# A Trainium2 trunk kernel: rounded weight parts by transfers of their own, one decay exponential a tile, and chunk inverses made one chunk ahead

## The chip, the cores and the metric

The kernel runs on one core of a Trainium2 chip. A core has a matrix engine (PE), a vector engine (DVE), a scalar engine (ACT), a third element engine (POOL) and a sync engine (SP) that only issues transfers; POOL issues transfers as well. The metric is the device time of one execution in microseconds; lower is better.

## The reference

What is computed is a two-layer trunk on 512 tokens of width 1024. Layer 0 is a time mix with a recurrent state and a convolutional FFN, layer 1 an attention (MLA) and another such FFN, each with a norm ahead of it and behind it. The change lies in the time mix, whose reference is, cut down (`xx` is the previous token minus this one, `yn` is `y` normalised by head):

```python
def _rwkv7_step(S, inp):
    r, w, k, v, a, b = inp
    sa = jnp.einsum('bhvk,bhk->bhv', S, a)
    S = S * w[:, :, None, :] + sa[..., None] * b[:, :, None, :] + v[..., None] * k[:, :, None, :]
    y = jnp.einsum('bhvk,bhk->bhv', S, r)
    return S, y
...
    xs = x[None] + xx[None] * mu[:, None, None, :]
    rkv = jnp.einsum('nbtd,nde->nbte', xs[:3], w_rkv)
    r, k, v = rkv[0], rkv[1], rkv[2]
    xw, xa, xg = xs[3], xs[4], xs[5]
    w_log = -jax.nn.softplus(-(w0 + jnp.tanh(xw @ w1) @ w2)) - 0.5
    decay = jnp.exp(-jnp.exp(w_log.astype(f32)))
    a = jax.nn.sigmoid(a0 + (xa @ a1) @ a2)
    g = jax.nn.sigmoid(xg @ g1) @ g2
    kk = (k * k_k).reshape(B, T, H, N).astype(f32)
    kk = kk / jnp.maximum(jnp.sqrt(jnp.sum(kk * kk, axis=-1, keepdims=True)), 1e-12)
    k = k * (1.0 + (a - 1.0) * k_a)
...
    seq = tuple(jnp.moveaxis(t, 1, 0) for t in (rh, wh, kh, vh, -kk, kk * ah))
...
    _, y = lax.scan(_rwkv7_step, S0, seq)
...
    bonus = (jnp.sum(rh * kh * r_k, axis=-1, keepdims=True) * vh).reshape(B, T, D)
    out = ((yn + bonus) * g).astype(x.dtype)
    return out @ w_o
```

The recurrence is computed in 8 chunks of 64 tokens. Inside a chunk it needs, for each head, the inverse of a unit triangular 64x64 matrix.

## The kernel before

Every large matmul is made of three: the weight and the activation are each split into a rounded part (`hi`) and a remainder (`lo`), and `mm3` (L131 to L133) adds lo·hi, hi·lo and hi·hi. `weight()` makes the two parts of a weight tile (1024 x 128, kept as two halves of 128x512, 256 KB each). For each half SP loads the raw half into one of 4 `wraw` places, ACT rounds it into `whi` (L82), and an engine subtracts to get `wlo` (L125): DVE in the time mix, POOL later. Six halves (three tiles) of `whi` and `wlo` are held at once. A tile's 8 steps over k are 24 matmuls.

The time mix fills the first 396 us. Its stages are, in order:

- the norm and `group(1, 0)`: three key tiles at once, fed as each of the 8 input tiles `xh`, `xl` is made; then two key tiles alone with the fp32 matmuls of the small projections (`inner`), then `group(1, 5)` with `lora` inside it, which makes the decay exponents `cs` and the rates in `bk`;
- `group(2, 0)`, two value tiles and `group(2, 5)`. Inside them, tile by tile, run `factors` (exponentials of `cs`: `ar[...,0]` holds exp of the previous token's exponent, so its 504-column exponential is read one column earlier and POOL sets the first column to one; `ar[...,1]` holds the unshifted one; `en` is the inverse; `ka` is an affine function of the rate), `key2` (the norm of `kr`, through `ps_kn`), and `ab` (small products for the triangular matrices, sent out to `s_ab`);
- `group(0, 0)` and five receptance tiles. Beside them runs `solve`, which is 2 halves of 31 steps of two DVE operations (`tm`, `s`) that invert the 32x32 diagonal blocks, the first half for chunks 0 to 3 and the second for chunks 4 to 7. `steps(n)` advances it by n steps in the code. Behind a half, transfers on POOL's queue (`s_xd`, `s_x1`) put the result in memory, and `fetch_x` loads what one chunk needs into `TB`, `LT` and `X1`. `inv1` and `inv2` (PE, tile `ps_i`, L659 and L668) complete that chunk's inverse. `bonus` (`ps_bo`) belongs to each receptance tile;
- 8 chunks: `u_step` (needs scores `lu`), scores of the next chunk (`ps_sc`), `u2_step` (needs the inverse of this chunk), `s_step`, `tokens` (`ps_tk`), `y_state`, `y_tokens`, `yt`. `gate` (`ps_g`) fills in. From chunk 5 on the first halves of the output projection `wo` fill in;
- the second halves of `wo`, 8 tiles back to back, and the first 4 weight tiles of the FFN (`win`), L131 to L133 again.

A scheduler sets the order on each engine from the order of the code and from priorities. Each engine then runs its list strictly in order, and so does each engine's transfer queue.

Of the kernel before, what the change touches and what calls it, by code (L numbers as in the profile page):

```python
# [9 lines left out]
F32 = mybir.dt.float32  # L10
# [46 lines left out]
class Trunk:  # L57
# [53 lines left out]
    def weight(self, src, n=D, m=P, prio=None, gain=None):  # L111


        out = []
        with self.tc.high_priority(offset=WP if prio is None else prio):
            for c in range(0, n, T):
                w = min(T, n - c)
                r = self.wraw(w)
                self.nc.sync.dma_start(out=r, in_=src[:, c:c + w])
                if gain is not None:  # L120
                    v = r.rearrange("q (k c) -> q k c", c=m)
                    self.tt(v, v, bcol(gain[:, c // m:(c + w) // m], m), ALU.mult)
                h, l = self.wset()
                self.act(h[:, :w], r)
                self.wlo.tensor_tensor(out=l[:, :w], in0=r, in1=h[:, :w].bitcast(F32), op=ALU.subtract)  # L125
                out += [(h[:, i:i + m], l[:, i:i + m]) for i in range(0, w, m)]
        return out
# [26 lines left out]
    def run(self):  # L154
# [40 lines left out]
        self.wlo = nc.vector  # L195
# [105 lines left out]
    def time_mix(self, nxt, cp, gt):  # L301
# [9 lines left out]
        ar = ap.tile([P, DT, NCH, 2, C], F32, name="ar")  # L311
# [7 lines left out]
        scan = t1.tile([P, T], F32, name="scan")  # L319
        w1 = lw.tile([P, D], F32, tag="w1", name="w1")  # L320
        g1 = [lw.tile([P, n], F32, tag=f"g{i}", name="g1") for i, n in enumerate((512, 768))]
        g1k = lambda o, n: g1[0][:, o:o + n] if o < 512 else g1[1][:, o - 512:o - 512 + n]
# [37 lines left out]
        def group(i, p0, pre=None, prio=GP, mid=None):  # L360

            lag = LAG
            w = [self.weight(I["wrkv"][i, p], prio=prio) for p in range(p0, p0 + 3)]
# [72 lines left out]
        qk = group(1, 0, first, prio=G0)  # L436
        for t, n in ((w1, I["w1"]), (g1[0], I["g1"][:, :512]), (g1[1], I["g1"][:, 512:]), (self.cst, I["cst"][:, :256]), (self.ident, I["cst"][:, 256:]), (scan, I["scan"])):
            nc.sync.dma_start(out=t, in_=n)
# [63 lines left out]
        nc.gpsimd.memset(ar[:, :, :, 0, 0:1], 1.0)  # L502
        self.use_log_exp()

        def factors(p):
            cp = cs[:, p, :]
            self.act(ar[:, p, :, 0, 1:C], c3(cp)[:, :, 0:C - 1], AF.Exp, scale=-CD)
# [3 lines left out]
            self.act(c3(ka), bk[:, p, :, 0, :], AF.Identity, scale=V("ka", p), bias=om[:, 48 + p:49 + p])  # L511
# [10 lines left out]
        def key2(p, kr, sq):  # L522
# [6 lines left out]
            self.tt(ar[:, p, :, 0, :], c3(kr), ar[:, p, :, 0, :], ALU.mult)  # L529
# [145 lines left out]
        def recept(p, q):  # L675
            nc.vector.tensor_copy(out=self.pc[:, :, p], in_=ar[:, p, :, 1, C - 1])
# [17 lines left out]
        for p in range(DT):  # L694
# [3 lines left out]
            steps((0, 0, 0, 7, 7, 3, 3, 3)[p])  # L698
            rp.append(recept(p, q))
            if p in (5, 7):  # L700
                fetch_x(p // 2 - 2)
                w = inv1(p // 2 - 2, bank2)
            if p == 6:
                inv2(0, w, bank2)
# [10 lines left out]
        inv2(1, w, bank2)  # L715
# [148 lines left out]
        for ch in range(NCH):  # L864
# [4 lines left out]
            if ch == 0:  # L869
                for p in range(4):  # L870
                    gate(p, 0)
            u2_step(ch, u)
            if n + 1 < NCH:
                fetch_x(n + 1)
# [7 lines left out]
            if ch < 3:  # L882
                steps((11, 12, 1)[ch])
# [3 lines left out]
            if ch in (0, 4):  # L887
                for p in range(0 if ch else 4, DT):
                    gate(p, ch // 4)
            if n + 1 < NCH:  # L890
                fetch_v(n + 1)
                w = inv1(n + 1)
            if 5 <= ch:
                fill(2)
            if n + 1 < NCH:
                inv2(n + 1, w)
# [34 lines left out]
        self.whs.append(self.open("whl2", bufs=WB - 6))  # L931

# [385 lines left out]
```

## Time and profile before

| | us |
|---|---|
| median of 3 runs | 1366.24 (1365.59 to 1367.61) |
| the profiled execution | 1370.63 |
| its span, first to last instruction | 1368.9 |
| PE busy | 1307.6 (96%) |
| DVE busy | 815.6 (60%) |
| ACT busy | 708.8 (52%) |
| POOL busy | 291.8 (21%) |
| mean granted PE clock | 0.975 |

The profile is one execution. Each engine's busy time is a share of the span, over stages with different limits, so the table says little on any one of them: views of a stretch of time tell which engine is full there and what the others wait for. A granted clock of 1.00 is 2.4 GHz and 0.50 is 1.2 GHz.

### The profile page before, as it was taken

To read this page: it belongs to the slowest core of one execution; us is meant where nothing else is said; L and a number is where in the kernel's file an instruction comes from. 1 tells how busy PE (TensorE), PEld (TensorE's weight loads), DVE (VectorE), ACT (ScalarE), POOL (GpSimd) and SP (SyncE) were. 2 spreads that over 40 slices of the span, in tenths; PEclk is the share of its full clock that TensorE was granted. 3 is DMA by queue.
4 is the path that set the end of the run, shared out by engine and by line. 5 is a ranking of instruction groups with operands and counts; after the bars stand their busy time and mean duration, and the time that the engine had idled before them with its cause. 6 is when DMAs were issued, how large, how long until landed. Compare 5 with 4: busy or idle time off the path is not lost.

```text
span 1368.9 us, 21882 instructions
## 1 busy us (share of the span) xinstructions
PE 1307.6 (96%) x8108; PEld 1077.8 (79%) x8108; DVE 815.6 (60%) x1512; ACT 708.8 (52%) x1353; POOL 291.8 (21%) x277
## 2 busy tenths in 40 slices
PE   7989997989999999999999999999999999999995
PEld 5467775878998888888888877777898888888885
DVE  7668787677797666665233887873566555541003
ACT  6699842567676444444232566674464444433231
POOL 0001421100010000000000241222355444444443
PEclk9999998899999999999999999999999999999998
DMA  6121593345533323223333145441223222233321
GB/s 208 61 77 63 169 260 90 77 106 132 170 124 124 100 94 100 98 95 92 94 98 94 44 119 116 106 106 47 78 77 101 100 93 100 99 90 93 97 77 62
DMA packets 111211, 141.41 MB, mean 103 GB/s; under 512 B 47552, under 2 KB 54592, under 8 KB 111104
## 3 DMA queue, kind: packets, MB, share of 16 engines
q1 hardware_dynamic: 107696, 129.52, 32.2%
q0 software_dynamic: 3408, 10.49, 2.4%
q8 instruction: 64, 1.05, 0.3%
q14 instruction: 43, 0.35, 0.1%
HBM read 120.31 MB, written 12.58 MB: 97 GB/s over the span
## 4 chain that ended last, share of the span: by engine, by line
PE 75%; DVE 11%; ACT 7%; issue 3%; DMA 2%; POOL 1%; SPq 0%; POOLq 0%; ACTq 0%; DVEq 0%
PE ps_in L132 11%; PE ps_in L133 11%; PE ps_in L131 11%; PE ps_out L131 7%; PE ps_out L133 7%; PE ps_out L132 7%; PE ps_pj L132 1%; PE ps_pj L131 1%; PE ps_pj L133 1%; PE ps_o L1185 1%; DVE wlo L125 1%; DVE x L220 1%; PE ps_sc L710 1%; PE ps_t L1169 1%; ACT whi L82 1%
## 5 line engine op out<-in xcount | busy, mean ns | idle before, releaser
L82 ACT ACTIVATE whi<-wraw 128x512 fp32r<-128x512 f32 (+2 forms) x411 | 249.6, 614 | 356.9 <-PE ps_out L133 132.9
L132 PE MATMUL ps_in<-xl,whi 128*128 128x512 f32 (+1 forms) x768 | 286.9, 374 | 4.8 <-DVE xl L88 4.8
L131 PE MATMUL ps_in<-xh,wlo 128*128 128x512 f32 (+1 forms) x768 | 286.8, 374 | 0.8 <-DVE wlo L125 0.7
L125 POOL TENSOR_TENSOR wlo<-wraw,whi 128x512 fp32r<-128x512 f32 (+2 forms) x176 | 221.8, 1266 | 304.4 <-ACT whi L82 299.0
L133 PE MATMUL ps_in<-xh,whi 128*128 128x512 f32 (+1 forms) x768 | 285.7, 373 | 0.0
L125 DVE TENSOR_TENSOR wlo<-wraw,whi 128x512 fp32r<-128x512 f32 x229 | 154.0, 679 | 92.7 <-ACT whi L82 90.8
L132 PEld LDWEIGHTS ps_in<-xl,whi 128*128 128x128 f32 x768 | 145.5, 190 | 31.3 <-DVE xl L88 6.3
L131 PEld LDWEIGHTS ps_in<-xh,wlo 128*128 128x128 f32 x768 | 145.3, 190 | 26.7 <-DVE wlo L125 0.9
L133 PEld LDWEIGHTS ps_in<-xh,whi 128*128 128x128 f32 x768 | 145.6, 190 | 24.8
L131 PE MATMUL ps_out<-hh,wlo 128*128 128x512 f32 (+1 forms) x396 | 146.6, 370 | 1.3 <-ACT mg L82 1.3
L133 PE MATMUL ps_out<-hh,whi 128*128 128x512 f32 (+1 forms) x396 | 145.3, 367 | 0.0
L132 PE MATMUL ps_out<-hl,whi 128*128 128x512 f32 (+1 forms) x396 | 144.1, 364 | 0.0
L85 DVE TENSOR_TENSOR macc<-macc,msq 128x512 f32<-128x512 f32 (+1 forms) x25 | 15.5, 619 | 136.1 <-ACT msq L82 136.1
L237 POOL TENSOR_TENSOR row<-row,msq 128x256 f32<-128x256 f32 x14 | 14.1, 1010 | 379.8 <-ACT msq L82 379.3
L131 PE MATMUL ps_pj<-xh,wlo 128*128 128x512 f32 x192 | 79.0, 430 | 8.6 <-ACT xh L82 6.7
L88 DVE SCALAR_TENSOR_TENSOR c<-gp,vec,c 128x512 f32<-128x512 f32 x88 | 72.6, 827 | 24.1 <-ACT c L82 22.7
L131 PEld LDWEIGHTS ps_out<-hh,wlo 128*128 128x128 f32 x396 | 74.4, 188 | 13.5 <-ACT mg L82 1.9
L133 PEld LDWEIGHTS ps_out<-hh,whi 128*128 128x128 f32 x396 | 74.3, 188 | 13.5
L132 PEld LDWEIGHTS ps_out<-hl,whi 128*128 128x128 f32 x396 | 74.3, 188 | 13.1
L132 PE MATMUL ps_pj<-xl,whi 128*128 128x512 f32 x192 | 77.2, 404 | 0.3 <-DVE xl L85 0.2
L133 PE MATMUL ps_pj<-xh,whi 128*128 128x512 f32 x192 | 76.5, 400 | 0.0
L85 DVE TENSOR_TENSOR u<-ps_in,row 128x512 f32<-128x512 f32 x44 | 30.3, 689 | 63.0 <-PE ps_in L133 63.0
(289 smaller groups left out, 2385.2 us busy)
## 6 DMA issues: line engine op xcount, KB each, us to landing
wraw<-in_win SPq DMA_DIRECT2D x176, 256.0 KB, 2.7
wraw<-in_wout SPq DMA_DIRECT2D x80, 256.0 KB, 2.6
wraw<-in_wrkv SPq DMA_DIRECT2D x48, 256.0 KB, 3.2
wraw<-in_wo SPq DMA_DIRECT2D x32, 256.0 KB, 2.9
x<-in_xT SPq DMA_DIRECT2D x16, 256.0 KB, 4.7
wraw<-in_ow SPq DMA_DIRECT2D x16, 256.0 KB, 3.1
s_ab<-ab POOLq DMA_DIRECT2D x16, 128.0 KB, 2.8
s_vt<-vT POOLq DMA_DIRECT2D x8, 256.0 KB, 2.8
```

Source lines behind the costliest of these rows:

```text
L82: self.nc.scalar.activation(out=out, in_=in_, func=func, **kw)
L85: self.nc.vector.tensor_tensor(out=out, in0=a, in1=b, op=op)
L88: self.nc.vector.scalar_tensor_tensor(out=out, in0=a, scalar=s, in1=b, op0=op0, op1=op1)
L125: self.wlo.tensor_tensor(out=l[:, :w], in0=r, in1=h[:, :w].bitcast(F32), op=ALU.subtract)
L131: mm(ps, lhsT=wl, rhs=xh, start=start, stop=False)
L132: mm(ps, lhsT=wh, rhs=xl, start=False, stop=False)
L133: mm(ps, lhsT=wh, rhs=xh, start=False, stop=stop)
L220: eng.tensor_tensor(out=xk, in0=xk, in1=mg, op=ALU.add)
L237: (self.nc.gpsimd if (h, k) in ACCP else self.nc.vector).tensor_tensor(out=self.acc2[:, c], in0=self.acc2[:, c], in1=sq, op=ALU.add)
L710: mm(qs[hd][:, p], lhsT=b, rhs=a, start=True, stop=True)
L1169: nc.tensor.transpose(out=q[:, o:o + P], in_=pr[i][:, j * P:(j + 1) * P], identity=t.ident)
L1185: nc.tensor.matmul(q[HALF[i], j * P:], lhsT=VT[pr // 4][j][:, c:c + 64], rhs=w, start=j == 0, stop=j == QB - 1)
```

## The change

1. `weight()`: while `self.cast` is set, `whi` is no longer rounded by ACT from the raw half. A transfer on POOL's queue reads the same half of the weight once more and rounds it on its way into `whi`. SP still loads the raw half, since `wlo` is made from it. This holds for the time mix's projections, the gates' weights, `wo` and the first four FFN tiles, 82 halves in all. The first group's six halves are loaded to places in the tile `art`, which is not yet used for anything else, and ACT rounds them as before. `w1`, `g1` and `scan` are put in `art` too.
2. `factors` makes one exponential of the decay, and the shifted one is gone. `before(p)` reads the unshifted one, one column earlier, after DVE has written ones into the first columns (128x8).
3. `ka` goes from ACT to DVE (`tensor_scalar`), the small copy `pc` from DVE to ACT.
4. `steps` before the chunks: 14 where there were 23, so the first half of `solve` ends there and one step of the second is done; the rest runs in chunks 0 to 2.
5. No inverse is made before the chunks. Chunk 0's is made inside chunk 0, after `u_step` and the next chunk's first scores, with the gates around it; each later chunk's at the end of the chunk before. Its `fetch_x` stands one chunk earlier than that. The second set of gates stands in chunk 4.

```diff
 
-    def weight(self, src, n=D, m=P, prio=None, gain=None):
+    def weight(self, src, n=D, m=P, prio=None, gain=None, raw=None):
 
...
         out = []
+        raw = raw or self.wraw
         with self.tc.high_priority(offset=WP if prio is None else prio):
...
                 w = min(T, n - c)
-                r = self.wraw(w)
+                r = raw(w)
                 self.nc.sync.dma_start(out=r, in_=src[:, c:c + w])
...
                 h, l = self.wset()
-                self.act(h[:, :w], r)
+                if self.cast and raw == self.wraw:
+
+                    self.nc.gpsimd.dma_start(out=h[:, :w], in_=src[:, c:c + w])
+                else:
+                    self.act(h[:, :w], r)
                 self.wlo.tensor_tensor(out=l[:, :w], in0=r, in1=h[:, :w].bitcast(F32), op=ALU.subtract)
...
             nc.vector.tensor_scalar(out=self.om[:, a:a + n], in0=self.vec[:, _VEC[nm]:_VEC[nm] + n], scalar1=-1.0, scalar2=1.0, op0=ALU.mult, op1=ALU.add)
-        self.wlo = nc.vector
+        self.wlo, self.cast = nc.vector, True
         f0, m1, f1 = FFN(self, 0), MLA(self), FFN(self, 1)
...
         ap = self.open("apool")
-        ar = ap.tile([P, DT, NCH, 2, C], F32, name="ar")
+        art = ap.tile([P, DT * NCH * 2 * C + P], F32, name="ar")
+        ar = art[:, :DT * NCH * 2 * C].rearrange("q (p c s t) -> q p c s t", p=DT, c=NCH, s=2)
         bk = ap.tile([P, DT, NCH, 2, C], F32, name="bk")
...
         lw = self.open("lw", side="right")
-        scan = t1.tile([P, T], F32, name="scan")
-        w1 = lw.tile([P, D], F32, tag="w1", name="w1")
-        g1 = [lw.tile([P, n], F32, tag=f"g{i}", name="g1") for i, n in enumerate((512, 768))]
-        g1k = lambda o, n: g1[0][:, o:o + n] if o < 512 else g1[1][:, o - 512:o - 512 + n]
+        scan = art[:, 7 * D:7 * D + T]
+        w1, g1 = art[:, 3 * D:4 * D], art[:, 4 * D:4 * D + 1280]
+        g1k = lambda o, n: g1[:, o:o + n]
         x = self.x
...
 
-        def group(i, p0, pre=None, prio=GP, mid=None):
+        def group(i, p0, pre=None, prio=GP, mid=None, raw=None):
 
             lag = LAG
-            w = [self.weight(I["wrkv"][i, p], prio=prio) for p in range(p0, p0 + 3)]
+            w = [self.weight(I["wrkv"][i, p], prio=prio, raw=raw) for p in range(p0, p0 + 3)]
             q = [self.bank("ps_pj") for _ in range(3)]
...
 
-        qk = group(1, 0, first, prio=G0)
-        for t, n in ((w1, I["w1"]), (g1[0], I["g1"][:, :512]), (g1[1], I["g1"][:, 512:]), (self.cst, I["cst"][:, :256]), (self.ident, I["cst"][:, 256:]), (scan, I["scan"])):
+        places = iter(range(2 * DT))
+
+        def staged(n):
+
+            o = next(places) * T
+            return art[:, o:o + n]
+        qk = group(1, 0, first, prio=G0, raw=staged)
+        for t, n in ((w1, I["w1"]), (g1, I["g1"]), (self.cst, I["cst"][:, :256]), (self.ident, I["cst"][:, 256:]), (scan, I["scan"])):
             nc.sync.dma_start(out=t, in_=n)
...
             kept(p, qk[p - 5])
-        nc.gpsimd.memset(ar[:, :, :, 0, 0:1], 1.0)
         self.use_log_exp()
 
+        def before(p):
+
+            nc.vector.memset(ar[:, p, :, 0, C - 1:C], 1.0)
+            o = p * NCH * 2 * C + C - 1
+            return art[:, o:o + NCH * 2 * C].rearrange("q (c s t) -> q c s t", s=2, t=C)[:, :, 0, :]
+
         def factors(p):
             cp = cs[:, p, :]
-            self.act(ar[:, p, :, 0, 1:C], c3(cp)[:, :, 0:C - 1], AF.Exp, scale=-CD)
             en = t1.tile([P, T], F32, tag="en", name="en")
...
             ka = t1.tile([P, T], F32, tag="ka", name="ka")
-            self.act(c3(ka), bk[:, p, :, 0, :], AF.Identity, scale=V("ka", p), bias=om[:, 48 + p:49 + p])
+            nc.vector.tensor_scalar(out=c3(ka), in0=bk[:, p, :, 0, :], scalar1=V("ka", p), scalar2=om[:, 48 + p:49 + p], op0=ALU.mult, op1=ALU.add)
             self.act(ar[:, p, :, 1, :], c3(cp), AF.Exp, scale=-CD)
...
             self.stt(kr, rv, 1e12, kr, ALU.min, ALU.mult)
-            self.tt(ar[:, p, :, 0, :], c3(kr), ar[:, p, :, 0, :], ALU.mult)
+            self.tt(ar[:, p, :, 0, :], c3(kr), before(p), ALU.mult)
             self.tt(bk[:, p, :, 0, :], c3(kr), bk[:, p, :, 0, :], ALU.mult)
...
         def recept(p, q):
-            nc.vector.tensor_copy(out=self.pc[:, :, p], in_=ar[:, p, :, 1, C - 1])
+            self.act(self.pc[:, :, p], ar[:, p, :, 1, C - 1])
             self.tt(ar[:, p, :, 1, :], c3(q), ar[:, p, :, 1, :], ALU.mult)
...
                 bonus(*rp.pop(0))
-            steps((0, 0, 0, 7, 7, 3, 3, 3)[p])
+            steps((0, 0, 0, 5, 5, 4, 0, 0)[p])
             rp.append(recept(p, q))
-            if p in (5, 7):
-                fetch_x(p // 2 - 2)
-                w = inv1(p // 2 - 2, bank2)
-            if p == 6:
-                inv2(0, w, bank2)
+        fetch_x(0)
+
         def score_mm(ch, g):
...
             bonus(*rp.pop(0))
-        inv2(1, w, bank2)
         gate_weights()
...
             if ch == 0:
+                w = inv1(0)
                 for p in range(4):
                     gate(p, 0)
+                inv2(0, w)
+                for p in range(4, DT):
+                    gate(p, 0)
+                fetch_x(1)
             u2_step(ch, u)
-            if n + 1 < NCH:
-                fetch_x(n + 1)
             if n < NCH:
...
             if ch < 3:
-                steps((11, 12, 1)[ch])
+                steps((11, 11, 40)[ch])
             y_tokens(ch, q)
...
                 yt(ch - 1)
-            if ch in (0, 4):
-                for p in range(0 if ch else 4, DT):
-                    gate(p, ch // 4)
+            if ch == 4:
+                for p in range(DT):
+                    gate(p, 1)
+            if n < NCH:
+                w = inv1(n)
             if n + 1 < NCH:
                 fetch_v(n + 1)
-                w = inv1(n + 1)
             if 5 <= ch:
                 fill(2)
+            if n < NCH:
+                inv2(n, w)
             if n + 1 < NCH:
-                inv2(n + 1, w)
+                fetch_x(n + 1)
             if ch == 6:
...
         self.whs.append(self.open("whl2", bufs=WB - 6))
+        self.cast = False
```

What this makes of the order is shown at three places. The first is PE at the end of the last receptance tile, where the chunks begin (`ps_i` the inverse, `ps_sc` scores, `ps_bo` the bonus, `ps_tk` tokens, `ps_u` the chunk's first product, `ps_g` gates). Before:

```order
L133 MATMUL ps_pj<-xh,whi 128x512
L710 MATMUL ps_sc<-ar,bk 128x128 x8
L659 MATMUL ps_i_2021<-s_1562 64x64 x8
L686 MATMUL ps_bo<-rkk,cst 128x512
L668 MATMUL ps_i_2087<-wi,s_1562 64x64 x8
L686 MATMUL ps_bo<-rkk,cst 128x512
L659 MATMUL ps_i_2166<-T_1793,s_1562 64x64 x8
```

After, from the same place, and then where the first inverse stands now:

```order
L701 MATMUL ps_bo<-rkk,cst 128x512
L722 MATMUL ps_sc<-ar,bk 128x128 x8
L701 MATMUL ps_bo<-rkk,cst 128x512 x2
L722 MATMUL ps_sc<-ar,bk 128x128 x8
L781 MATMUL ps_tk<-ident,bk 128x64 x16
L789 MATMUL ps_u<-v,lu_2166 64x64
```

```order
L722 MATMUL ps_sc<-ar,bk 128x128 x5
L674 MATMUL ps_i_2257<-s_1550 64x64 x8
L136 MATMUL ps_g<-gt,wlo 128x256
L137 MATMUL ps_g<-gxl,whi 128x256
L138 MATMUL ps_g<-gt,whi 128x256
L569 MATMUL ps_g<-gt,whi 128x256
```

Sixteen scores, two bonuses, the 16 token transposes and all of `ps_u` stand ahead of the first `ps_i` now, where 8 scores stood; the gates stand right behind it.

The second place is ACT inside `group(2, 0)`, around the factors of one tile (`krv` the key norm, `hm` and `xh` the group's own inputs). Before:

```order
L82 ACTIVATE ar<-cs 128x8x63
L82 ACTIVATE xh<-xs 128x512
L82 ACTIVATE hm<-h,om 128x512
L82 ACTIVATE en<-cs 128x512
L82 ACTIVATE ka<-bk,om,vec 128x512
L82 ACTIVATE xh<-xs 128x512
L82 ACTIVATE ar<-cs 128x8x64
L82 ACTIVATE kr<-bk,vec 128x512
L82 ACTIVATE ksq<-bk,vec 128x512
L82 ACTIVATE krv<-ps_kn,tiny 128x512
L82 ACTIVATE hm<-h,om 128x512
L82 ACTIVATE krv<-krv 128x512
```

After:

```order
L82 ACTIVATE en<-cs 128x512
L82 ACTIVATE ar<-cs 128x8x64
L82 ACTIVATE xh<-xs 128x512
L82 ACTIVATE hm<-h,om 128x512
L82 ACTIVATE ksq<-bk,vec 128x512
L82 ACTIVATE krv<-ps_kn,tiny 128x512
L82 ACTIVATE xh<-xs 128x512
L82 ACTIVATE krv<-krv 128x512
```

The 504-column exponential (128x8x63) and `ka` are gone from the list, and no cast of weights stands among the rest any more. Earlier on ACT, in `group(1, 5)`, one `en` stands ahead of rates that are still to come, and with it two table loads that were not there:

```order
L82 ACT_TABLE_LOAD
L82 ACTIVATE en<-cs 128x512
L82 ACT_TABLE_LOAD
L82 ACTIVATE sg<-ps_lo,vec 128x512
L82 ACTIVATE bk<-ps_lo,vec 128x8x64
```

Before, one table load stood between the last of the rates (`sg`, `bk`) and the first `en`; now an `en` is drawn in among them, and there are three.

The third place is POOL's queue, from its first transfers on. Before:

```order
L541 DMA s_ab<-ab 128x4x64 x2
L417 DMA s_vt<-vT 128x512 x2
L541 DMA s_ab<-ab 128x4x64 x2
L417 DMA s_vt<-vT 128x512 x2
L541 DMA s_ab<-ab 128x4x64 x2
```

After:

```order
L127 DMA whi<-in_wrkv 128x512 x19
L556 DMA s_ab<-ab 128x4x64 x2
L127 DMA whi<-in_wrkv 128x512 x2
L422 DMA s_vt<-vT 128x512
L127 DMA whi<-in_wrkv 128x512
L422 DMA s_vt<-vT 128x512
L127 DMA whi<-in_wrkv 128x512
```

The weights' transfers stand among those that send results of ACT out, in one queue; a transfer there waits behind the ones ahead of it.

## Rows read from the trace of the kernel before

**Rows 1.** Windows of the time mix; columns in its first row
```profile
core 0: us, PE busy (x) PEld busy (x) DVE busy (x) ACT busy (x) POOL busy (x), PEclk, DMA share, GB/s
0.00:72.00 72.00, 63.71 (x226) 36.72 (x227) 48.27 (x74) 48.77 (x77) 1.65 (x11) 0.95 0.38 128
72.00:152.00 80.00, 71.82 (x414) 53.13 (x414) 58.61 (x92) 77.02 (x133) 11.62 (x16) 0.96 0.27 88
152.00:168.00 16.00, 16.00 (x168) 12.35 (x163) 13.87 (x22) 13.23 (x25) 6.33 (x9) 1.00 0.62 188
168.00:200.00 32.00, 31.06 (x152) 25.67 (x151) 27.49 (x58) 16.82 (x30) 7.83 (x13) 1.00 0.92 253
200.00:224.00 24.00, 24.00 (x102) 18.82 (x101) 21.98 (x52) 7.42 (x11) 3.81 (x8) 1.00 0.45 130
224.00:264.00 40.00, 30.90 (x306) 23.83 (x306) 22.39 (x57) 14.47 (x29) 6.80 (x12) 0.70 0.35 80
264.00:296.00 32.00, 27.65 (x592) 24.46 (x588) 27.63 (x66) 22.46 (x50) 1.10 (x2) 1.00 0.37 87
296.00:360.00 64.00, 61.21 (x1155) 56.49 (x1154) 45.90 (x84) 45.97 (x103) 0.00 (x0) 1.00 0.56 153
360.00:396.00 36.00, 36.00 (x319) 35.88 (x316) 30.61 (x63) 27.31 (x63) 0.00 (x0) 1.00 0.50 155
```

**Rows 2.** Groups of ACT, 72 to 152 us: busy, mean ns, idle before
```profile
L82 ACT ACTIVATE whi<-wraw 128x512 fp32r<-128x512 f32 x19 | 11.6, 627 | 0.0
...
L82 ACT ACTIVATE ka<-bk,om,vec 128x512 f32<-128x512 f32 x7 | 5.6, 806 | 0.0
...
L82 ACT ACTIVATE ar<-cs 128x504 f32<-128x504 f32 x8 | 5.0, 619 | 0.0
...
L82 ACT ACT_TABLE_LOAD x2 | 2.6, 1283 | 0.0
```

**Rows 3.** What PE waited for, 72 to 152 us (us, times, longest)
```profile
PE ps_kn L524 <- ACT ksq L82: 3.6, 1, 3.6
PE ps_kn L524 <- ACT krv L82: 2.2, 1, 2.2
PE ps_pj L131 <- DVE wlo L125: 1.9, 3, 1.0
```

**Rows 4.** What PE waited for, 224 to 300 us
```profile
PE ps_i L659 <- DMA s<-s_x: 8.3, 1, 8.3
PE ps_i L659 <- issue: 1.5, 1, 1.5
```

**Rows 5.** Chain of waits, 222 to 240 us: start us, us, what
```profile
223.18 2.10 ACT s L82
...
232.43 1.69 DMA s<-s_x
```

**Rows 6.** What PE waited for, 0 to 30 us
```profile
PE ps_pj L131 <- ACT xh L82: 6.3, 1, 6.3
```

**Rows 7.** Groups of DVE, 72 to 152 us
```profile
L125 DVE TENSOR_TENSOR wlo<-wraw,whi 128x512 fp32r<-128x512 f32 x18 | 11.9, 682 | 3.6 <-ACT whi L82 3.5
...
L676 DVE COPY pc<-ar 128x8 f32<-128x8 f32 x8 | 2.4, 295 | 1.4 <-ACT ar L82 1.4
```

**Rows 8.** Issues of `s_vt` on POOL: ns min/median/max
```profile
L417 POOL DMA_DIRECT2D s_vt<-vT x8: 552/552/555, 130.7 to 177.8; - x8
```

**Rows 9.** Transfers, 72 to 152 us: KB each, median us to landing
```profile
s_vt<-vT POOLq DMA_DIRECT2D x4, 256.0 KB, 2.3
```

**Rows 10.** Projections alone, 200 to 224 us: PE, PEld, DVE, ACT
```profile
200.00:224.00 24.00, 23.11 (x96) 17.73 (x95) 2.73 (x4) 0.00 (x0) 1.00 0.45 130
```

**Rows 11.** Transfers, 160 to 224 us
```profile
wraw<-in_wrkv SPq DMA_DIRECT2D x11, 256.0 KB, 4.3
```

**Rows 12.** Output projection matmuls alone, 360 to 396 us: PE, PEld, ACT
```profile
360.00:396.00 36.00, 35.01 (x285) 34.43 (x285) 8.32 (x22) 1.00 0.50 155
```

**Rows 13.** Transfers of those 36 us: packets, MB, share of 16 engines
```profile
q1 hardware_dynamic: 3017, 5.50, 49.4%
```

## The prediction

> **What bounds the kernel now.** I read the windows table first [rows 1], to see in which stretch of the time mix PE is not full, or full at a low granted clock. PE is nearly full in most; what is lost lies in three. From 72 to 152 us it is busy 71.8 of 80 at a clock of 0.96: 8.2 us idle, and about 0.04 x 71.8 = 2.9 of slow work, 11.1 in all. From 224 to 264 it is busy 30.9 of 40 at 0.70: 9.1 idle and 0.30 x 30.9 = 9.3 slow. From 264 to 296 it is idle 4.4. Behind 296 there is little to gain: 2.8 us of 64, and nothing in the last 36.
>
> Next, who is late there. In the first stretch ACT is busy 77.0 of 80 [rows 1], and its list [rows 2] shows no idle time ahead of any group: ACT is the bound, and PE's waits are for what ACT makes [rows 3], 3.6 us for `ksq`, 2.2 for `krv`, and 1.9 for `wlo`, which waits for ACT's cast in its turn. In the second stretch PE waits 8.3 us for one transfer, the inverse's data, and 1.5 behind it [rows 4]. The chain [rows 5] tells the story: `solve`'s first half ends, ACT copies (2.10 us at 223.18), and only at 232.43 does the last load begin, since the result goes out to memory and back. The first `ps_i` stands behind 8 scores only, so PE has nothing else; after the wait the clock is low. DVE works beside it, 22.4 + 27.6 = 50.0 us of the 72 from 224 to 296 [rows 1].
>
> **The change part by part.**
>
> *Start.* The first projection waits 6.3 us for ACT's first `xh` [rows 6]. In the order of the changed kernel all six casts of the first group stand ahead of `xh`, as six did before, but five now stand behind the norm. One more operation on that path is 0.68 us on DVE (`wlo`) [rows 7]; I take +0.6, with ends -1 and +1.5.
>
> *72 to 152 us.* ACT loses 17 of the 19 casts (two belong to the small weights, which keep theirs): 17 x 0.627 = 10.7; eight exponentials, 5.0; seven `ka`, 5.6 [rows 2]. It gains two table loads, 2 x 1.283 = 2.6, and eight `pc`, no row of ACT; as on DVE 0.295 each [rows 7], 2.4. Net 16.3, so ACT falls to 60.7 of the present 80. DVE has 58.6 now [rows 1] and gets seven `ka`, between 0.295 and 0.69 by the other DVE rows, at most 4.8, loses 2.4 of `pc` and gets small memsets of less: about 61. So neither is the bound any more and PE is, with its 11.1 us of loss as the most that can be had. The three waits of [rows 3] make 7.7; the clock, with no idle stretch of 3.6 us left, may give back 2.9: 10.6 together.
>
> Against that stands a longer way to a weight. Now `whi` needs no place until the raw half is there, and a cast (0.63) and `wlo` (0.68) follow. After the change the transfer itself must wait until PE releases the place, then takes 0.55 to issue [rows 8] and 2.3 to land [rows 9], and `wlo` 0.68: 3.5 us against 1.3. A half lasts PE 12 matmuls of 23.11/96 = 0.24, 2.9 us [rows 10]. In the single tiles six halves are in hand, 17 us, and nothing shows. At the end of a group all three tiles end together, and the order has 12 matmuls between the last release and the first need: 3.5 - 2.9 = 0.6 a half at best, and if transfers queue behind one another 1.5 or so. Two group ends lie in this stretch; I take 2.5 off. **Forecast -8**, with ends -11 and 0 (all of it eaten).
>
> *152 to 224 us.* PE is full, so only loss is possible. Eleven raw halves are loaded from 160 to 224 [rows 11]; each is now read twice. One costs all sixteen transfer engines about 0.494 x 36 / 21 = 0.85 us, by the 5.50 MB (21 halves of 0.262) in the last stretch [rows 12, 13]. That is 9.4 us more in a stretch where their share is 0.92 for 32 us and 0.45 for 24 (free: 2.6 + 13.2) [rows 1]. It fits, late. Two more group ends are here. **+2**, ends 0 and +9.
>
> *224 to 296 us.* The inverse of chunk 0 now stands behind sixteen scores, two bonuses, the token transposes and `ps_u`, work that PE does today after the wait. So the 8.3 and the 1.5 are covered; where that cover is gone, they are back. With no long idle stretch the clock should not fall, 9.3 us. But then DVE is what is late next: its 50.0 us here include solve's second half, which must end before chunk 4, and none of it goes away. 72 - 50 = 22 is all that DVE leaves, and PE's own loss, 9.1 + 9.3 + 4.4 = 22.8, says the same. A serial chunk does not run DVE full: I take the waits (9.8) and somewhat under half of the clock (4.2). **-14**, ends -22 and -5.
>
> *The rest of the chunks.* Nothing before 360 changes but places; 0. Solve's last steps stand in chunk 2, and chunk 4's inverse at the end of chunk 3; the way out and back (11 us in [rows 5], from 223.2 to 234.1) has about a chunk to hide in.
>
> *The last 36 us.* `wo` matmuls take 35.01/285 = 0.123 [rows 12], so a half lasts 1.47 us, and needs 2 x 0.85 = 1.7 us of the transfer engines. 21 halves fall short by 0.23 each, 4.8; six stand ready. **+1.5**, ends 0 and +8 (the issues on POOL too, 0.55 each [rows 8], hide).
>
> A page of the Trainium skill speaks against sending weights this way: SBUF - State Buffer (the box on the "DVE blocks DMA" trap) says that a DMA from POOL's queue cannot get its descriptors while DVE runs a 2-port operation, as an fp32 copy from SBUF to SBUF is, and gives 3.1 us where 0.62 was needed. The moved `ka` would be such an operation. The trace does not show it: the eight `s_vt` issues took 552, 552 and 555 ns (least, median, most) [rows 8] while DVE was busy 73% of the stretch, though with few copies in it. By the page's figures eight such delays would cost at most 8 x 2.5 = 20 us of waiting in transfers, an estimate, most of it hidden.
>
> **Sum.** 0.6 - 8 + 2 - 14 + 1.5 = -17.9. The profiled execution took 1370.6, so it would take 1352.7; it is 4.4 above the median of 1366.2, and I set the same difference on the median: **1348.3 us**.
>
> **Rivals.**
> 1. *The transfers are late and eat the first stretch* (8 becomes 0). For it: the longer way to a weight, and one queue for weights and for ACT's results, where a weight waits behind an `s_ab` that waits for ACT. Against it: a landing of 2.3 us. 0.6 + 0 + 2 - 14 + 1.5 = -9.9: 1356.
> 2. *The inverse's wait returns inside chunk 0* (or DVE is the bound sooner): 14 becomes 5, the clock stays low. For it: DVE must end solve's first half with everything else it has there. 0.6 - 8 + 2 - 5 + 1.5 = -8.9: 1357.
> 3. *Both*: -0.9: 1365, no change that shows.
> 4. *All goes well*: -11 - 22 + 0.6 = -32: 1334.
> 5. *A DVE lock on POOL's descriptors*, priced by rows: each of eight `ka` holds a weight back by its own length, 0.69 at most, 5.5 us of the 8: 1354.
> 6. *Slower: POOL's queue carries one weight at a time in the output projection.* Then a half costs its landing, 2.3 us, or 4.3 where traffic is dense [rows 11], against 1.47. 24 halves (8 tiles of `wo` and 4 of the FFN) at 4.3 - 1.47 = 2.8 are +68, at 2.3 +20; without the 1.5 the sum is -19.4, so it decides from (19.4/24 + 1.47) = 2.3 us a half. At 3 us: 24 x 1.53 = 37 - 19 = +17: 1384. Against it: 21 hardware transfers passed in 36 us, and a landing time is not a spacing.
> That the change does not do what it says, the order excludes.
>
> **How the numbers follow.** Chances: forecast 0.46 (its own range 1340 to 1354), rival 1 0.17, rival 2 0.12, both 0.05, all well 0.07, lock 0.04, slower 0.09. Faster by more than 0.2% (2.7 us, what a measurement of this kernel can tell from no change): 0.46 + 0.17 + 0.12 + 0.07 + 0.04 = 0.86; within 0.05; slower 0.09. The range leaves out the slower case, "both", and about half of "all well", 0.18 in all: 1335 to 1364.
>
> **What would show each step.** ACT under 65 of 80 us between 72 and 152, with no wait of PE for `ksq` or `krv`: the first term. PE's waits for `wlo` there, over 4 us: rival 1. PE at a clock near 1.00 from 224 on with no wait over 2 us for `s_x`, chunk 3 some 14 us sooner against the end of the last projection: the fourth term; a wait of `ps_i` in chunk 0 is rival 2. A `ps_wo` waiting for `wlo` is rival 6. The forecast is wrong if the transfers land in more than about 5 us where a group ends, or if DVE fills the chunks.

## The result: slower

The changed kernel took 1381.6 us (median of 4, 1378.9 to 1387.8) where the kernel before took 1366.9: a ratio of 1.011, 95% interval 1.007 to 1.015. The forecast was 1348. The profiled execution of the change took 1387.8 us, 17.1 more than that of before, where the medians differ by 14.7.

I laid the two traces side by side by events of PE: the end of a projection tile, of a chunk, of a weight tile. How far the change is behind (+) or ahead (-) at each, in us, gives the terms of the sum as they came out:

| up to | before | after | behind | term | forecast |
|---|---|---|---|---|---|
| end of the first group | 38.7 | 40.0 | +1.3 | +1.3 | +0.6 |
| end of the second value tile alone | 143.8 | 149.6 | +5.8 | +4.5 | -8 |
| end of the last receptance tile | 224.8 | 237.9 | +13.2 | +7.4 | +2 |
| end of the last chunk | 366.8 | 372.8 | +6.0 | -7.2 | -14 |
| first 4 FFN weight tiles, about | 423.1 | 437.6 | +14.5 | +8.5 | +1.5 |
| last instruction | 1368.9 | 1386.0 | +17.1 | +2.6 | 0 |

The last 2.6 lie behind the code that is changed. A position comes from one profiled execution each: `e6` below, whose code is the change's up to the chunks, is +10.4 at the last receptance tile, so a difference of 3 us between two kernels' positions says little by itself. The windows of the change, which answer to [rows 1] (PE, PEld, DVE, ACT, POOL busy, granted clock, transfers' share, GB/s):

```profile
72.00:152.00 80.00, 71.99 (x414) 51.23 (x414) 61.60 (x94) 65.05 (x112) 19.72 (x33) 0.98 0.51 151
...
168.00:200.00 32.00, 29.21 (x171) 24.42 (x170) 19.37 (x41) 10.49 (x18) 13.28 (x22) 1.00 1.02 262
200.00:224.00 24.00, 20.35 (x73) 15.25 (x74) 17.43 (x37) 1.45 (x2) 4.39 (x8) 0.86 0.80 234
224.00:264.00 40.00, 35.19 (x258) 27.73 (x258) 30.98 (x81) 15.44 (x29) 11.50 (x20) 0.83 0.52 136
264.00:296.00 32.00, 28.27 (x630) 24.94 (x628) 29.15 (x72) 20.38 (x44) 0.00 (x0) 1.00 0.35 77
...
360.00:396.00 36.00, 33.76 (x371) 32.12 (x370) 21.86 (x41) 13.67 (x36) 9.52 (x18) 1.00 0.95 284
```

ACT did fall, from 77.0 to 65.1 of the 80 us from 72 to 152, and PE gained nothing by it. From 168 to 224 us, where PE had been full, it is idle 6.4 us: the transfer engines are full for the first 32 of them (1.02) and at 0.80 after that. In the last row their share is 0.95, where it was 0.50, and PE idles 2.2.

What PE waits for from 72 to 152 us, against [rows 3]:

```profile
PE ps_pj L136 <- DVE wlo L130: 4.0, 5, 2.2
PE ps_vt L428 <- ACT krv L82: 2.0, 1, 2.0
```

The waits for `ksq` are gone, and those for `wlo` have grown from 1.9 to 4.0 us. The weights' transfers there, and from 160 to 224 us (KB each, median us to landing; [rows 9, 11] before):

```profile
whi<-in_wrkv POOLq DMA_DIRECT2D x20, 256.0 KB, 3.8
wraw<-in_wrkv SPq DMA_DIRECT2D x18, 256.0 KB, 3.1
```

```profile
whi<-in_wrkv POOLq DMA_DIRECT2D x16, 256.0 KB, 4.9
wraw<-in_wrkv SPq DMA_DIRECT2D x12, 256.0 KB, 5.5
...
s<-s_ab SPq DMA_DIRECT2D x4, 256.0 KB, 7.1
```

3.8 us and then 4.9, where I had put 2.3 by `s_vt`; and the loads for the triangular matrices, `s<-s_ab`, take 7.1. One chain shows what that does. It runs from 188 to 204 us (start, length, what):

```profile
187.99 7.45 DMA whi<-in_wrkv
...
195.86 0.69 DVE wlo L130
...
199.71 0.41 DVE s L85
...
200.91 0.69 DVE wlo L130
...
202.77 0.75 DVE rkk L88
...
203.65 2.04 PE ps_bo L701 x2
```

A rounding transfer takes 7.45 us. DVE's `wlo` waits for it at 195.86. DVE runs its list in order, so `solve`'s steps and `rkk`, the bonus's input, come behind it, and `rkk` ends at 203.5. PE, whose list has the bonus in the middle of a projection, stands still.

That transfer is not the whole delay, and not the larger part. DVE's list a little earlier (start, length; in brackets how long DVE stood and for what), in the change and then, one line, in `e1`, which is the change without the rounding transfers:

```profile
188.76 0.19 DVE L85 TENSOR_TENSOR tm<-s 128x31 f32<-128x31 f32 x1 [3.76 <-DMA s<-s_ab]
...
194.50 0.69 DVE L130 TENSOR_TENSOR wlo<-wraw,whi 128x512 fp32r<-128x512 f32 x1 [2.26 <-PE ps_pj L136]
```

```profile
178.49 0.18 DVE L85 TENSOR_TENSOR tm<-s 128x31 f32<-128x31 f32 x1
```

These `tm` are `solve`'s first step. DVE stands 3.8 us ahead of it for a load of `s_ab`, then 2.3 for a place that PE holds, and 0.4 for the transfer of 7.45. The first step is 10.3 us later than in `e1`, and the first `rkk` 10.1 (202.8 for 192.6): against `e1` the delay is there when `solve` starts.

What PE waits for from 196 to 290 us, and the clock in some windows of that stretch (PE busy, clock, share, GB/s):

```profile
PE ps_bo L701 <- DVE rkk L88: 7.6, 2, 6.4
PE ps_tk L781 <- DVE sign L750: 3.6, 1, 3.6
```

```profile
200.00:204.00 4.00, 0.35 (x1) 0.79 1.10 362
204.00:208.00 4.00, 4.00 (x8) 0.50 0.98 264
...
244.00:248.00 4.00, 0.84 (x16) 0.83 0.75 169
248.00:252.00 4.00, 3.53 (x31) 0.50 0.92 235
252.00:256.00 4.00, 4.00 (x42) 0.50 0.78 178
256.00:260.00 4.00, 4.00 (x24) 0.50 0.15 27
```

The 6.4 us are most of the loss of the third term, with half clock behind them. The second stop comes at the start of the chunks. DVE there:

```profile
241.27 0.74 DVE L88 SCALAR_TENSOR_TENSOR rkk<-ar,vec,bk 128x512 f32<-128x512 f32 x1
245.72 0.09 DVE L627 MEMSET s<- 128x32 f32 x1 [3.71 <-POOL s L626]
246.93 0.19 DVE L85 TENSOR_TENSOR tm<-s 128x31 f32<-128x31 f32 x1 [1.12 <-ACT s L82]
247.03 0.68 DVE L85 TENSOR_TENSOR vTr<-ps_bo,vTr 128x512 f32<-128x512 f32 x1
...
248.33 0.14 DVE L750 COPY sign<-cst 128x1 f32<-128x1 f32 x1
```

DVE stands 3.7 us before it writes the ones for `solve`'s second half, for POOL's clearing, and 1.1 more for ACT's copy. The last bonuses (`vTr`) and the `sign` that PE's token transposes wait for are behind that in its list; PE's clock is at 0.50 from 248 to 260. The output projection shows the last loss, transfers from 360 to 410 us against [rows 13]:

```profile
q1 hardware_dynamic: 4533, 8.26, 51.5%
q0 software_dynamic: 3740, 6.81, 47.2%
...
whi<-in_wo POOLq DMA_DIRECT2D x19, 256.0 KB, 5.3
wraw<-in_wo SPq DMA_DIRECT2D x18, 256.0 KB, 5.4
```

Both queues together hold 99% of sixteen engines, and a half lands after 5.3 us.

### The profile page after: what moved, and what is told of

Same layout as the page of the kernel before. It is cut to its first block, busy times and chain, and to the rows that moved or that the text cites. A ratio compares the mean times of both kernels' runs of the same rounds, so it can differ in the third digit from the quotient of the medians.

```text
span 1386.0 us, 21956 instructions
## 1 busy us (share of the span) xinstructions
PE 1312.0 (95%) x8108; PEld 1078.1 (78%) x8108; DVE 816.5 (59%) x1520; ACT 659.7 (48%) x1263; POOL 337.2 (24%) x360
## 4 chain that ended last, share of the span: by engine, by line
PE 67%; issue 12%; DVE 9%; DMA 6%; ACT 3%; POOL 2%; POOLq 0%; SPq 0%; DVEq 0%; ACTq 0%
PE ps_in L137 11%; PE ps_in L138 11%; PE ps_in L136 11%; PE ps_out L136 7%; PE ps_out L138 7%; PE ps_out L137 7%; DMA whi<-in_wrkv 3%; PE ps_o L1203 1%; DVE x L225 1%; PE ps_t L1187 1%; DVE wlo L130 1%; PE ps_pj L137 1%; PE ps_pj L136 1%; PE ps_pj L138 1%; POOL whi L127 1%
## 5 line engine op out<-in xcount | busy, mean ns | idle before, releaser
L82 ACT ACTIVATE whi<-wraw 128x512 fp32r<-128x512 f32 (+2 forms) x321 | 194.6, 610 | 329.5 <-PE ps_out L138 132.6
L136 PE MATMUL ps_pj<-xh,wlo 128*128 128x512 f32 x192 | 78.4, 426 | 11.8 <-ACT xh L82 7.2
```

Source lines behind the costliest of these rows:

```text
L82: self.nc.scalar.activation(out=out, in_=in_, func=func, **kw)
L136: mm(ps, lhsT=wl, rhs=xh, start=start, stop=False)
```

## The experiments

Each run is given with its ratio to the kernel before on the same chip and the 95% interval; positions are those of the table above. The kernel before took 1369.5 to 1371.6 us beside these runs and 1366.9 beside the change, so kernels are compared by their ratios.

**The parts apart.** `e1` is the change with one word of it undone:

```diff
-        self.wlo, self.cast = nc.vector, True
+        self.wlo, self.cast = nc.vector, False
```

> The changed kernel with no rounding transfers: ACT casts every weight half again, each weight is read once; the single exponential, the moved ka and pc, the staged first group and the new order of solve and inverses stay. Theory T (reading each weight twice fills the transfer engines, once from 168 to 200 us and once in the output projection, and a late hi part holds up DVE, which runs in order, and PE behind it): both losses vanish, the chunks keep their 7 us of gain, so 1358 us (1352 to 1364), under the kernel before. Rival R (solve's first half, now ended later in the code, is what makes PE wait for DVE; the transfers don't matter): it stays at 1375 or more.

Measured 1355.1 us, ratio 0.988 (0.984 to 0.992): R falls. It is level with the kernel before at the last receptance tile (-0.0), 15.3 ahead at the last chunk, and stays there. So the rounding transfers alone make the difference between -15.4 and +17.1 us at the last instruction: -0.3, 5.2, 8.3, 8.1, 8.5 and 2.7 by the terms of the table. Its windows:

```profile
168.00:200.00 32.00, 31.54 (x153) 25.82 (x151) 28.36 (x62) 15.13 (x27) 7.17 (x11) 1.00 0.94 253
200.00:224.00 24.00, 24.00 (x101) 18.70 (x100) 20.66 (x49) 8.73 (x13) 6.16 (x11) 1.00 0.54 156
224.00:264.00 40.00, 37.08 (x643) 31.14 (x643) 35.05 (x86) 24.72 (x56) 4.10 (x8) 1.00 0.42 91
```

`e2` puts the transfers alone into the kernel before:

```diff
-                self.act(h[:, :w], r)
+                if self.cast and not own:
+                    self.nc.gpsimd.dma_start(out=h[:, :w], in_=src[:, c:c + w])
+                else:
+                    self.act(h[:, :w], r)
```

> The kernel before with only the rounding transfers (the first group is cast by ACT, as in the change). T: it loses the 7 to 9 us between 168 and 215 us and some 9 in the last 40 us of the time mix, without the chunks' gain: 1385 us (1378 to 1392). R: 1370 or less, or a gain.

Measured 1392.9, ratio 1.016 (1.012 to 1.020), 0.9 past the end of T's range: +11.2 at the last receptance tile, +24.7 at the FFN's first tiles. `e3` has solve's steps and the inverses moved alone:

```diff
-            steps((0, 0, 0, 7, 7, 3, 3, 3)[p])
+            steps((0, 0, 0, 5, 5, 4, 0, 0)[p])
...
-                steps((11, 12, 1)[ch])
+                steps((11, 11, 40)[ch])
```

> The kernel before with only solve's steps and the inverses moved, as in the change. T: 1360 us (1355 to 1364), 7 us off between the last projection and the last chunk, and no wait of PE for the bonus's input in the receptance tiles. R: that wait is there, and the time is 1372 or more.

Measured 1358.5, ratio 0.991 (0.988 to 0.994): T. `e4` has the single exponential, `ka` and `pc` alone:

```diff
-            self.act(ar[:, p, :, 0, 1:C], c3(cp)[:, :, 0:C - 1], AF.Exp, scale=-CD)
...
-            self.tt(ar[:, p, :, 0, :], c3(kr), ar[:, p, :, 0, :], ALU.mult)
+            self.tt(ar[:, p, :, 0, :], c3(kr), before(p), ALU.mult)
```

> The kernel before with only the single decay exponential, ka on DVE and pc on ACT (and the small table scan kept in the tile ar, for room). T: ACT, full from 72 to 152 us, loses some 9 us of work there; PE's waits for the key norms shrink: 1363 us (1359 to 1367). Rival: DVE, which gets ka and the ones, or the added table loads take it back: 1367 and no difference.

Measured 1363.9 with a spread of 1356.4 to 1369.1, ratio 0.995 (0.992 to 0.997). A gain, but of 1.6 us only at the last receptance tile; the rest comes in chunk 0, where the inverse's data are waited for 4.7 us, not 8.3, since `solve`'s first step comes at 178.5, 5.6 us earlier. Of PE's waits (60 to 224 us) `ksq` shrinks from 3.6 and `krv` stays:

```profile
PE ps_kn L529 <- ACT ksq L82: 2.4, 1, 2.4
PE ps_ab L542 <- ACT krv L82: 2.3, 1, 2.3
```

**Where the transfers cost.** `e5` ends them before `group(2, 5)`, `e6` before the output projection, `e12` leaves them out between `group(0, 0)` and the chunks. Each sets `self.cast` at that place:

```diff
+        self.cast = False
         qv = group(2, 5, mid=lambda k: keyed(9 + k // 2) if k in (0, 2) else None)
```

> The changed kernel with the rounding transfers kept only up to the second value tile alone (until about 150 us); from group(2, 5) on ACT casts. T (double reads fill the transfer engines from 168 us on and in the output projection): both losses vanish, 1364 us (1358 to 1369). Rival L (the transfers' late start behind PE's release and POOL's queue costs wherever they are used): about half of the 15 us of loss stays, 1372.

Measured 1357.3, ratio 0.990 (0.988 to 0.993), better than T asked and equal to `e1` within their intervals: the first 20 transfers, the last of them issued at 126.9 us, neither gain nor lose anything that shows.

> The changed kernel with ACT's casts again for the output projection and the FFN's first tiles, transfers elsewhere in the time mix. T: the 9 us between the last chunk and the first FFN tiles go, the loss from 168 to 215 stays: 1373 us (1369 to 1377). Rival: the last stage is late for what the chunks leave behind, not for the transfers: 1380.

Measured 1374.9, ratio 1.004 (1.002 to 1.006): the last stage's 8.5 go (+2.6 at the last chunk and at the FFN's first tiles), the rest stays, as T says.

> The changed kernel with ACT's casts for the receptance tiles and the gates' weights alone (about 180 to 230 us), transfers before and behind. T (the transfer engines were full there already): the 8 us from 197 to 213 us and the low clock in chunk 0 go, the output projection's 9 stay: 1368 us (1364 to 1372). Rival (the backlog comes from the value tiles before it): 1378.

Measured 1370.6, ratio 1.001 (0.9995 to 1.003): T. Over the receptance tiles it loses 1.2 us (from +2.3 to +3.5) where the change loses 9.0 (from +4.2 to +13.2), and it is -9.1 at the last chunk; then the output projection takes 9 back. PE's waits there:

```profile
PE ps_bo L702 <- DVE rkk L88: 1.3, 1, 1.3
...
PE ps_tk L782 <- DVE sign L751: 0.2, 1, 0.2
```

**Traffic or late start.** `e8` keeps the rounding transfer and drops the raw load:

```diff
-                self.nc.sync.dma_start(out=r, in_=src[:, c:c + w])
+                if not one:
+                    self.nc.sync.dma_start(out=r, in_=src[:, c:c + w])
```

> The changed kernel in which a weight that is rounded by a transfer is not read a second time: the raw half isn't loaded, and wlo is hi minus hi, so zero (the remainders of these weights are left out). The late start of a transfer stays, the doubled traffic goes. T: the losses from 168 to 215 us and in the output projection go with the traffic: 1365 us (1358 to 1369). L (late start): 1376 or more.

Measured 1367.2, spread 1361.4 to 1370.4, ratio 0.998 (0.996 to 0.999): in T's range, and still 1% above `e1`. From the last chunk to the FFN's tiles it loses 3.8 where the change loses 8.5; over the receptance tiles 4.9 (from -0.4 to +4.5), where the change loses 9.0. So the doubled traffic is about half of each loss. The other half is a `hi` part that is still late: DVE stands up to 2.3 us for one in the receptance tiles, and PE 1.9 for a `wlo` in the FFN's tiles. Whether it is late because the transfer can start only when PE releases the place, or because it lands slowly, isn't shown; from 168 to 200 us the transfer engines are as full here as in the change. Its share at both places, and the landing in the output projection:

```profile
168.00:200.00 32.00, 28.68 (x134) 23.34 (x133) 24.69 (x54) 7.50 (x13) 10.93 (x18) 0.95 1.03 249
...
360.00:396.00 36.00, 33.78 (x264) 33.17 (x263) 29.80 (x65) 14.94 (x39) 10.61 (x20) 0.95 0.58 156
```

```profile
whi<-in_wo POOLq DMA_DIRECT2D x14, 256.0 KB, 3.1
```

**The port lock.** `e7` puts `ka` back on ACT.

```diff
-            nc.vector.tensor_scalar(out=c3(ka), in0=bk[:, p, :, 0, :], scalar1=V("ka", p), scalar2=om[:, 48 + p:49 + p], op0=ALU.mult, op1=ALU.add)
+            self.act(c3(ka), bk[:, p, :, 0, :], AF.Identity, scale=V("ka", p), bias=om[:, 48 + p:49 + p])
```

> The changed kernel with ka on ACT again. Rival K (DVE's one-operand operation on fp32 data in SBUF locks POOL out of writing descriptors, so that weights land late): the hi parts land in 2.3 us from 72 to 152 where 3.8 is seen, and the time falls by 5, to 1377. T: they land as before, and the time is the same within 3 us, 1382.

Measured 1385.0, ratio 1.010 (1.008 to 1.012), as the change. The hi parts land there in 3.4 us, where the change has 3.8 and K asked for 2.3:

```profile
whi<-in_wrkv POOLq DMA_DIRECT2D x20, 256.0 KB, 3.4
```

So K falls: the time does not drop, and the change's 3.8 us are not `ka`'s doing but for 0.4 at most (in `e8`, with `ka` on DVE and less traffic, they land in 3.4 too). The Trainium skill's page SBUF - State Buffer (box on the "DVE blocks DMA" trap) has such an operation lock POOL out of writing descriptors while it runs. A hold of `ka`'s own length, 0.55 us, can't be told from none here.

**The chunks' missing half.** `e11` let `solve` pause behind its first half, to take its second half out of DVE's list ahead of the last bonuses.

```diff
                 nc.gpsimd.dma_start(out=self.s_x1[g], in_=sA[:64].rearrange("q a b -> q (a b)"))
+                yield
...
-                nc.vector.memset(sX.rearrange("q a b -> q (a b)")[:, ::33], 1.0)
+                (nc.gpsimd if g else nc.vector).memset(sX.rearrange("q a b -> q (a b)")[:, ::33], 1.0)
```

> The changed kernel, transfers and all, with solve paused in the same way. Theory H (with the transfers late, DVE stands still for solve's second half, with the last bonuses and the scores' masks behind it; PE then waits 3.6 us and its clock is at 0.50 for about 12 us): that wait and the low clock go, 5 to 8 us off the 1382, 1375 us (1372 to 1378). Rival: PE then waits for another late thing at the same place (the last bonus's input), 1381.

Measured 1399.9, ratio 1.021 (1.018 to 1.024). The pause also moved ACT's copy of the second half's input behind `fetch_x(0)`, which writes over it; the second half is computed from other data, and PE waits 13.9 us for the result ahead of chunk 4. It answers nothing. `e13` mends that: the copy and the clearing stay ahead of the pause.

```diff
                 if g == 1:
-                    self.act(sA, lX)
-                    nc.gpsimd.memset(s4[:, 1], 0.0)
+                    yield
...
+                if g == 0:
+                    self.act(sA, lX)
+                    nc.gpsimd.memset(s4[:, 1], 0.0)
```

> The changed kernel, transfers and all, with solve paused behind its first half: the copy and the clearing that the second half needs stay where they are, its ones are written by POOL and its first step stands in chunk 0, so none of it is ahead of the last bonuses on DVE. (The run e11 meant this, but put the copy behind the first fetch too, which overwrites what it reads, and so lengthened chunk 2; it answers nothing.) Theory H: the 3.6 us wait of PE behind DVE and the 12 us at half clock go, 5 to 8 us off, 1375 us (1372 to 1378). Rival: another late thing takes its place, 1381.

Measured 1382.7, ratio 1.009 (1.006 to 1.012): the rival. The wait for `sign` is gone, and 4.8 us for the inverse's data stand in its place:

```profile
PE ps_bo L703 <- DVE rkk L88: 8.2, 3, 6.2
PE ps_i L676 <- DMA T<-s_xd: 4.8, 1, 4.8
```

So DVE's standstill was one face of it. What lies ahead of both is that `solve`'s first half ends late. ACT's copy behind it starts in the change, and in `e1`, at (start, length):

```profile
240.26 1.99 ACT L82 ACTIVATE s<-s 64x1024 f32<-64x1024 f32 x1 [0.44 <-DVE s L85]
```

```profile
218.56 2.09 ACT L82 ACTIVATE s<-s 64x1024 f32<-64x1024 f32 x1 [2.20 <-DVE s L85]
```

The change's last projection ends at 237.9 and that of `e1` at 224.7: the copy starts 2.4 us behind it in the one and 6.1 ahead of it in the other. Over the kernels with the new order, and the kernel before: the end of chunk 0 (its `s_step`), counted from the last projection's end, and the gain on the kernel before from there to the last chunk:

| kernel | half ends, against last projection | chunk 0 ends behind it | chunks' gain |
|---|---|---|---|
| before | -1.6 | 37.7 | |
| e9 | -6.2 | 18.4 | 17.0 |
| e14 (below) | -6.2 | 18.4 | 11.2 |
| e1 | -6.1 | 18.4 | 15.3 |
| e5 | -4.1 | 19.3 | 15.8 |
| e8 | -3.1 | 26.7 | 11.9 |
| e12 | -2.2 | 22.4 | 12.6 |
| e3 | -1.4 | 23.7 | 10.7 |
| change | +2.4 | 28.4 | 7.2 |
| e7 | +2.9 | 26.8 | 11.8 |
| e6 | +3.1 | 29.0 | 7.8 |
| e13 | +3.3 | 28.8 | 8.2 |

The end of chunk 0 goes with that margin, but for `e8`, where PE waits 2.9 us for the last bonuses' input. The gain up to the last chunk follows less well, since later chunks have stops of their own: `e14` waits 6.0 us for the second half's data, and in the change PE's clock is at 0.79 from 296 to 312 us; `e7`, with the half as late, gains 11.8. No run moves the half's end by itself, so that it is the cause is argued from this table and not shown.

**A faster version.** `e9` is `e1` with the first group loaded through the usual four places:

```diff
-        qk = group(1, 0, first, prio=G0, raw=staged)
+        qk = group(1, 0, first, prio=G0)
```

> The changed kernel with no rounding transfers, and the first group's raw halves loaded through the four usual places, not through the tile ar. Theory S: the staged loads put five casts between the norm and the first input and cost 1.5 us at the first group's end (40.3 us against 38.7); without them that end is at 38 to 39, and the time 1.5 under the run e1, 1353.5 us. Rival: the loss is made up later anyway, 1355.

Measured 1351.4 (1350.4 to 1352.3), ratio 0.986 (0.984 to 0.987): the lowest of all, in an interval that overlaps that of `e1`; the first group ends at 37.9 where `e1` has 40.3. `e10` and `e14` are `e9` with the pauses of `e11` and `e13`.

> As e9, and solve pauses once its first half is sent out, so that none of the second half (its first step, and the ones that DVE writes, which POOL writes here) stands ahead of the last bonuses on DVE. Without the transfers DVE is in time there (no wait of PE for it in e1), so the same as e9 within 2 us: 1353 us.

> The run e9 (no rounding transfers, first group unstaged) with solve paused in the same way. There PE did not wait at that place, so the same as e9 within 2 us: 1351 us.

`e10` took 1367.1, ratio 0.997 (0.995 to 0.999), with the overwritten input of `e11`. `e14` took 1354.0, ratio 0.989 (0.986 to 0.992), 3 us above `e9` where no more than 2 were expected: the pause gains nothing, and its own wait, 6.0 us for the second half's data, comes in its place.

## Why the prediction was wrong, step by step

- **Start.** Sign and cause right, size 1.3 for 0.6; with the staging undone (`e9`) the first group ends 0.8 earlier than before, as it does in `e4`.
- **72 to 152 us** is the step that failed most: -8 was forecast, +4.5 came, outside its ends of -11 and 0. That ACT is full there was read rightly, and its relief came out at 12.0 us where I had 16.3. The error was to credit PE with its waits as soon as ACT has room. From the first group's end to the second value tile PE gained 0.7 us in `e4`, with the exponentials and `ka` alone, 0.7 in `e1`, and 0.2 in `e8`, where ACT is rid of the casts too and is busy 68.6 of the 80. The likely reason, not shown by a run, is that the waits hang on one chain per tile (`ksq`, the norm on PE, `krv` twice on ACT, `kr`), whose length is little shorter when ACT is less busy. So of the 12.5 us by which this term missed, 7.3 are a relief that was worth 0.7, and 5.2 are what the transfers cost beside it. For I priced a transfer's landing at 2.3 by results sent out while the transfer engines were at 0.27; here their share is 0.51, weights take 3.8, and `wlo` is waited for 4.0 us. That is rival 1. Its queueing half, a weight behind an `s_ab` that waits for ACT, happened too: POOL (start, length, wait) stands 10 us ahead of the `s_ab`, but the `whi` behind it has no part in PE's waits from there to 152 us.

```profile
124.64 1.54 POOL L556 DMA_DIRECT2D s_ab<-ab  x2 [10.03 <-ACT ab L82]
126.17 0.57 POOL L127 DMA_DIRECT2D whi<-in_wrkv  x1
```

Most of the 5.2 us fall in one tile, the second value tile alone: 16.3 us in the change, 12.5 before. The wait there is the 2.0 us for `krv`, and ACT (start, length, wait) tells what holds it:

```profile
138.93 0.69 ACT L82 ACTIVATE krv<-ps_kn,tiny 128x512 f32<-128x512 f32 x1 [1.97 <-DMA s_ab<-ab]
```

`krv` is written to one of three places that it shares with `ksq` and `ab`, and the place is free only when an `ab` has been sent out. The two transfers that send it take 5.4 and 5.1 us to land in the change, 2.4 each in the kernel before. Behind the wait the clock is at 0.61 from 140 to 144 us; both together are the 3.8 us by which the tile is longer. `e6`, `e11`, `e12` and `e13` show the same wait, 1.8 to 1.9 us, with landings of 4.9 to 5.5; `e5`, whose transfers have ended by then, and `e1` have 2.4 to 2.5 and no wait in that tile. So it is the transfers again, this time through a result that could not leave.

- **152 to 224 us**: +7.4 for +2, inside the bound of +9. I added the doubled traffic to the free share of the whole stretch ("it fits, late") and did not ask what late costs. Late meant a load of `s_ab` that let `solve` start 10.3 us later than in `e1`, 7.45 us for a weight, DVE's list in order behind both, and half clock after PE's stop. With ACT's casts there (`e12`) 1.2 of the 9.0 us of the receptance tiles are left.
- **224 to 296 us**: -7.2 for -14, and the mechanism was right: without the rounding transfers it is -15.3 (`e1`), with the new order alone -10.7 (`e3`). That DVE must end solve's first half in time was named in rival 2; I did not see that term three feeds it. The two were added as if they were apart.
- **The last stage**: +8.5 for +1.5, just past the upper bound of +8. The working was right (1.7 us of transfers for 1.47 of PE); I let six ready halves pay for it, and took no price for a late `hi` part, which is about half (`e8`). Rival 6, one weight at a time, did not happen: 5.3 us to landing, but both queues full.
- **The sum.** The measured 1381.6 lies near the slower rival's 1384 by number, not by its mechanism. It is rivals 1 and 2 with the bounds of two more terms, which my range treated as four separate chances. They have one cause in the main, the rounding transfers: without them the same kernel is 15.4 us ahead at its end, near the forecast's 17.9, though the gain comes in the chunks and none of it is there by 152 us.

What stays open: how much of the late `hi` parts is a late start and how much a slow landing; and which wait carries the second term in `e2` and `e7`. These lose 4.0 and 5.1 us from the first group's end to the second value tile by other waits in that tile (0.7 us for `bk`; 1.7 for `ab`) and by what comes before it. Every kernel whose transfers go on into `group(2, 5)` loses 2.0 to 5.1 there (the change, `e2`, `e6`, `e7`, `e11`, `e12`, `e13`), `e5`, where they end ahead of it, 0.5, and `e8`, where weights are read once, gains 0.2.

## What to carry to other kernels

Moving work from an engine to a transfer was paid twice here: in traffic where the transfer engines were already full, which slowed every other load and store as well, and in results that came late for engines that run in order. Before such a move, read the transfers' share in each stretch, and ask which engine has a late result in its list, what else stands behind it there, and which places stay taken until a transfer out has landed. And an engine that is full need not be what the others lose by: ACT was busy 96% of a stretch, lost 12 us of its work, and PE gained next to nothing.

## What the runs showed of the hardware

- A rounding transfer of 256 KB from POOL's queue landed, in the median, in 3.4 to 3.8 us at a transfers' share of 0.36 to 0.51 (`e8`, the change; 72 to 152 us), in 4.9 from 160 to 224 us and 5.3 from 360 to 410, where the share was 0.90 and 0.99; single ones took up to 7.8.
- With both queues full, from 360 to 410 us, the plain loads took 25.8 us of all sixteen engines for 8.26 MB and the rounding transfers 23.6 for 6.81, so 3.1 and 3.5 us a MB.
- Short stops of PE cost twice: behind waits of 6.4 and 3.6 us the granted clock stood at 0.50 from 204 to 208 and from 248 to 260 us, with PE busy nearly all of that time.
- `pc` on ACT took 0.22 us and `ka` on DVE 0.55.
